# Attention outputs with the values stationary and the gate turned instead of the product

## The chip, the cores and the metric

The kernel runs on one core of a Trainium2 chip. The metric is the device time of one execution in microseconds (us). Three runs of the kernel before took 927.52, 927.58 and 927.73 us; the median is 927.58 us.

## The reference

A two-layer decoder trunk over 256 positions with a width of 2048, all f32. Each layer does the same five things; only the mixers differ.

```python
h = rmsnorm(x, norm_g)
q, k, v, ..., gate = split_cols(h @ w_in, SPLIT)
y = concatenate([mixer_1(q, k, v), mixer_2(q, k, v)])   # 16 heads of 128
x = x + (y * silu(gate)) @ w_out
```

- Layer 0: 10 heads A attend over 64 keys that a top-k search picked (one key/value head shared by all), 6 heads B over dilated windows. Both end in `softmax(logits) @ v`.
- Layer 1: 8 heads C (stick-breaking: weights `exp(log_sigmoid(z) + tail)`, not normalised) and 8 heads D (forgetting attention, a softmax).

A last RMSNorm ends the trunk. The change concerns the last steps of each head, from the weights of the keys to `y * silu(gate)`.

## The kernel before, in words

**Projections.** The 256 tokens are two blocks of 128 (`th` 0 and 1). A *job* multiplies the normed tokens by one group of columns of `w_in` or `w_out`, up to 512 wide: usually one head's q, k, v and gate, or two heads A with their gates. A job runs over 16 k-tiles of 128. To get f32 accuracy from a faster format, operands are cut into a high part (`F32R`, printed as f32 in the profile) and a low part, and each product is three matmuls: high times high, low times high, high times low (`products`, L302 to L308; 6 matmuls a k-tile). Weights come by DMA in pieces of four k-tiles; ScalarE writes their high part (`whi`, L269) and VectorE the low part (`wlo`, L270), two k-tiles (a half) at a time and three halves ahead, into four buffers.

**Order.** The schedule is written by hand: instructions reach each engine's queue in program order, and each queue runs in order. The attention of a head is a Python generator that runs beside the projection of the following job. `tick` (L293) counts projected columns. One tick is a k-tile of a 512-wide job, and two to three k-tiles of the narrow jobs K, F1 and G1 count for one or two. At each tick `advance` lets every generator whose count has run out emit its next stage; `yield n` asks for n ticks until the next one. A stage's TensorE work therefore stands between two k-tiles of the projection.

**A head.** Right after its job, ScalarE and VectorE take q, k, v and gate out of PSUM. For B (`head_b`, L484) they are rotated, and `u` is the gate times (1 + tanh). For C and D, `scaled_qk` (L649) and `vg1` (L657) scale q and k, take two exponentials, copy v, and form `u` with a reciprocal (L666) and two products (L669). C1 is the exception: its q and k come from job F1, its v and gate from job G1. Then

- q and k are turned by TensorE (`turn`, L364) and cut (`qk_turned`, L367 to L376);
- scores: one f32 matmul for the first token block, three split ones for the second (L407 to L410, L712 and L713);
- B, D and A (`softmax_head`): the masked minimum on VectorE (L414), the exponential on ScalarE (L416), three transposes of the weights (L419), a copy (L421);
- C (`stick_head`, L708): softplus, a triangular product for the running sums (L726 to L729), an exponential (L732); its weights are made turned already;
- outputs (`weigh_out`, L387): three f32 matmuls with the turned weights stationary and the values moving (L390 to L392), the product with 1/sum, norm and gate (L396), a transpose of y (L398), and the cut into `yh` and `yl` (L400, L401), from which the output projection reads.

The heads of a pair A run two ticks apart. The jobs of layer 0 are B0, K, I0, I1, B1 to B3, five pairs of A, B4 and B5, then the output projection P0 to P3. Those of layer 1 are C0, F1, G1, C2 to C7, D0 to D7, Q0 to Q3.

Of the kernel before, what the change touches and what calls it, by code (L numbers as in the profile page):

```python
# [11 lines left out]
OP = mybir.AluOpType  # L12
# [147 lines left out]
def trunk(ctx, tc, x, xT, g1, w0, wo0, w1, wo1, bf, gf, consts, rope, out):  # L160
# [216 lines left out]

    def three(o, ah, al, bh, bl):
        nc.tensor.matmul(o, ah, bh, start=True, stop=False)  # L379
        nc.tensor.matmul(o, ah, bl, start=False, stop=False)  # L380
        nc.tensor.matmul(o, al, bh, start=False, stop=True)  # L381
# [5 lines left out]
    def weigh_out(pT, vs, u, sc, kt):  # L387

        po = pa.tile([P, SEQ], F32, name="o", tag="o", bufs=1)
        nc.tensor.matmul(po[:, 0:P], pT[0], vs[0], start=True, stop=True)  # L390
        nc.tensor.matmul(po[:, P:SEQ], pT[1], vs[0], start=True, stop=False)  # L391
        nc.tensor.matmul(po[:, P:SEQ], pT[2], vs[1], start=False, stop=True)  # L392
        y = hp.tile([P, SEQ], F32, name="y", tag="y", bufs=2)
        for th in range(NT):
            t = slice(th * P, (th + 1) * P)
            nc.vector.scalar_tensor_tensor(y[:, t], po[:, t], sc[:, th:th + 1], u[:, t], op0=OP.mult, op1=OP.mult)  # L396
        yield 2 if kt == KT - 1 else 3
        pt = turn([y[:, 0:P], y[:, P:SEQ]])  # L398
        yh, yl = ys
        nc.scalar.activation(yh[:, kt, :], pt[:, 0:SEQ], AF.Copy)  # L400
        nc.vector.tensor_tensor(yl[:, kt, :], pt[:, 0:SEQ], yh[:, kt, :].bitcast(F32), op=OP.subtract)  # L401

    def softmax_head(qk, nb, vs, u, rs, kt):

        q0, k0, q1h, q1l, kh, kl = qk
        pS = pa.tile([P, 384], F32, name="s", tag="s", bufs=1)
        nc.tensor.matmul(pS[:, 0:P], q0, k0, start=True, stop=True)  # L407
        three(pS[:, P:384], q1h, q1l, kh, kl)
        sn = hp.tile([P, 384], F32, name="sn", tag="sn", bufs=2)
        nm = hp.tile([P, NT], F32, name="nm", tag="nm", bufs=2)  # L410
        pr = hp.tile([P, 384], F32, name="pr", tag="pr", bufs=2)
        l = hp.tile([P, NT], F32, name="l", tag="l", bufs=2)
        for th, s in BLK:
            nc.vector.tensor_tensor_reduce(sn[:, s], pS[:, s], nb[:, s], op0=OP.add, op1=OP.min, scale=1.0,  # L414
                                           scalar=3.0e38, accum_out=nm[:, th:th + 1])
            nc.scalar.activation(pr[:, s], sn[:, s], AF.Exp, scale=-1.0, bias=nm[:, th:th + 1],  # L416
                                 accum_out=l[:, th:th + 1])
        yield 3
        pt = turn([pr[:, 0:P], pr[:, P:SEQ], pr[:, SEQ:384]])  # L419
        pT = hp.tile([P, 384], F32, name="pT", tag="pT", bufs=2)  # L420
        nc.scalar.activation(pT, pt[:, 0:384], AF.Copy)  # L421
        sc = hp.tile([P, NT], F32, name="sc", tag="sc", bufs=2)
        nc.vector.reciprocal(sc, l)
        nc.vector.tensor_tensor(sc, sc, rs, op=OP.mult)
        yield 2
        yield from weigh_out([pT[:, i * P:(i + 1) * P] for i in range(3)], vs, u, sc, kt)
# [140 lines left out]

    def best():
# [8 lines left out]
        nc.vector.tensor_tensor(nbA, nbA, nmask, op=OP.max)  # L577

# [4 lines left out]
    def heads_a(ps, h):  # L583
# [7 lines left out]
        for th in (1, 0):  # L591
# [65 lines left out]
    def vg1(ps, o):  # L657
        v = hp.tile([P, NT, P], F32, name="v", tag="v")
        u = hp.tile([P, SEQ], F32, name="u", tag="u")
        e = hp.tile([P, SEQ], F32, name="e", tag="tg")  # L660
        for th in range(NT):
            t = slice(th * P, (th + 1) * P)
            nc.scalar.activation(e[:, t], ps[th][:, o + P:o + 256], AF.Exp, scale=nr1[:, th:th + 1])
            nc.scalar.activation(v[:, th], ps[th][:, o:o + P], AF.Copy, scale=r1[:, th:th + 1])
        nc.vector.tensor_scalar(e, e, 1.0, 3.0e38, op0=OP.add, op1=OP.min)
        nc.vector.reciprocal(e, e)  # L666
        for th in range(NT):
            t = slice(th * P, (th + 1) * P)
            nc.vector.tensor_tensor(u[:, t], ps[th][:, o + P:o + 256], e[:, t], op=OP.mult)  # L669
# [38 lines left out]
    def stick_head(qk, v, u, kt):  # L708
# [7 lines left out]
        sp = hp.tile([P, 384], F32, name="sp", tag="pr")  # L716
# [16 lines left out]
        yield 3
        yield from weigh_out([w[:, 256:384], w[:, P:256], w[:, 0:P]], [v[:, 0], v[:, 1]], u, r1, kt)

    def head_c(ps, h):
        qk = scaled_qk(ps, 0)
        v, u = vg1(ps, 256)
        yield 2
        t = qk_turned([qk[:, 384:512], qk[:, 256:384], qk[:, 0:P], qk[:, P:256]])  # L740
        yield 2
        yield from stick_head(qk_of(t), v, u, h)

    def head_cf(ps, qk):
        v, u = vg1(ps, 0)
        yield 2
        t = qk_turned([qk[:, 384:512], qk[:, 256:384], qk[:, 0:P], qk[:, P:256]])
        yield 2
        yield from stick_head(qk_of(t), v, u, 1)

    def head_d(ps, h):
# [5 lines left out]
        yield from softmax_head(qk_of(t), biases[h], [v[:, 0], v[:, 1]], u, r1, HC + h)  # L757
# [133 lines left out]
```

## Time and profile before

| | |
|---|---|
| median of the runs | 927.58 us |
| profiled execution | 927.35 us |
| its span | 925.6 us |
| TensorE busy | 916.7 us (99%) |
| VectorE busy | 591.4 us (64%) |
| ScalarE busy | 474.6 us (51%) |
| DMA | 168.77 MB, 182 GB/s over the span |

The span runs from the first to the last instruction; the profiled execution's own time contains it. "Busy" is the time in which an engine has an instruction under way. Matmuls overlap in the pipeline, so the mean of a group of matmuls (392 ns for one of 512 columns) is longer than the distance between two starts. In the timeline, starts are in us from the span's start, the second column is the duration, and x2 means two instructions merged. An f32 matmul shows as two instructions.

### The profile page before, as it was taken

Reading aid. Unit: us, or ns where it says so; the run is one execution under the profiler, and the core shown is the slowest. Engines: PE = TensorE matmul, PEld = TensorE weight load, DVE = VectorE, ACT = ScalarE, POOL = GpSimd, SP = SyncE. Lnnn points to the kernel's source line nnn. Section 1 sums busy time; section 2 is a strip of 40 time slices with the busy share of each in tenths; the row PEclk is TensorE's granted clock in tenths of the full one; section 3 lists DMA queues with packets and bytes.
Section 4 is the critical chain, followed back from the end, with each engine's and each line's share of the span. In section 5 each row is a group of like instructions: output and inputs, shape, how many; then the busy total and the mean of one; then the engine's idle time right before and its main releaser. Section 6 shows DMA issues by size and latency. Waiting matters only on the chain.

```text
span 925.6 us, 12017 instructions
## 1 busy us (share of the span) xinstructions
PE 916.7 (99%) x4541; PEld 770.8 (83%) x4541; DVE 591.4 (64%) x982; ACT 474.6 (51%) x804; POOL 48.5 (5%) x68
## 2 busy tenths in 40 slices
PE   9999999999999999999999999999999999999996
PEld 6988888888888888888898888888888888888886
DVE  7667888656666555555477666666766666665563
ACT  7645554554454455444465555555555444554450
POOL 0021100000000000000000000000000000001110
PEclk9999999999999999999999999999999999999999
DMA  9954454545444554555356454444655555455542
GB/s 359 366 189 156 164 182 166 182 154 182 141 163 153 182 181 169 187 187 186 94 204 217 183 175 156 160 158 173 236 182 188 182 167 174 176 182 182 182 182 91
DMA packets 27322, 168.77 MB, mean 182 GB/s; under 512 B 3168, under 2 KB 3712, under 8 KB 9344
## 3 DMA queue, kind: packets, MB, share of 16 engines
q1 hardware_dynamic: 25920, 164.70, 49.8%
q0 software_dynamic: 768, 2.12, 0.8%
q10 hardware_dynamic: 576, 1.19, 0.3%
q8 instruction: 35, 0.57, 0.3%
q14 instruction: 23, 0.19, 0.1%
HBM read 165.89 MB, written 2.11 MB: 182 GB/s over the span
## 4 chain that ended last, share of the span: by engine, by line
PE 97%; issue 1%; DMA 0%; DVE 0%; ACT 0%; POOL 0%; POOLq 0%; DVEq 0%; ACTq 0%
PE pj L305 30%; PE pj L306 29%; PE pj L308 29%; PE tp L364 3%; PE o L392 1%; PE o L390 1%; PE o L391 1%; PE s L407 1%; PE s L380 1%; PE s L379 1%; PE s L381 1%; DMA w0yh<-in_w_in_dram 0%; PE tp L635 0%; PE s L556 0%; PE s L557 0%
## 5 line engine op out<-in xcount | busy, mean ns | idle before, releaser
L270 DVE TENSOR_TENSOR wlo<-raw,whi 128x1024 fp32r<-128x1024 f32 (+3 forms) x300 | 356.4, 1202 | 190.7 <-ACT whi L269 189.8
L305 PE MATMUL pj<-whi,xh 128*128 128x512 f32 (+3 forms) x992 | 387.3, 392 | 0.2 <-ACT whi L269 0.2
L306 PE MATMUL pj<-whi,xl 128*128 128x512 f32 (+3 forms) x992 | 377.0, 382 | 0.0
L269 ACT ACTIVATE whi<-raw 128x1024 fp32r<-128x1024 f32 (+3 forms) x300 | 302.5, 1025 | 131.0 <-PE pj L306 125.9
L308 PE MATMUL pj<-wlo,xh 128*128 128x512 f32 (+3 forms) x992 | 297.7, 381 | 0.0
L308 PEld LDWEIGHTS pj<-wlo,xh 128*128 128x128 f32 x992 | 183.5, 188 | 36.7 <-DVE wlo L270 0.2
L305 PEld LDWEIGHTS pj<-whi,xh 128*128 128x128 f32 x992 | 186.9, 188 | 31.3 <-ACT whi L269 1.2
L306 PEld LDWEIGHTS pj<-whi,xl 128*128 128x128 f32 x992 | 187.1, 189 | 30.3
L305 PE MATMUL pj<-whi,yh 128*128 128x512 f32 (+1 forms) x248 | 96.2, 388 | 0.0
L306 PE MATMUL pj<-whi,yl 128*128 128x512 f32 (+1 forms) x248 | 94.9, 383 | 0.0
L308 PE MATMUL pj<-wlo,yh 128*128 128x512 f32 (+1 forms) x248 | 76.7, 383 | 0.0
L308 PEld LDWEIGHTS pj<-wlo,yh 128*128 128x128 f32 x248 | 46.6, 188 | 9.2
L306 PEld LDWEIGHTS pj<-whi,yl 128*128 128x128 f32 x248 | 46.7, 188 | 8.5
L305 PEld LDWEIGHTS pj<-whi,yh 128*128 128x128 f32 x248 | 46.7, 188 | 8.5
L416 ACT ACTIVATE pr<-sn,nm 128x128 f32<-128x128 f32 (+1 forms) x48 | 21.5, 449 | 47.6 <-DVE nm L414 47.6
L400 ACT ACTIVATE yh<-tp 128x256 fp32r<-128x256 f32 x32 | 12.3, 384 | 56.9 <-PE tp L364 56.7
L401 DVE TENSOR_TENSOR yl<-tp,yh 128x256 fp32r<-128x256 f32 x32 | 13.6, 424 | 26.1 <-ACT yh L400 25.3
L430 ACT ACTIVATE sq<-xs 128x512 f32<-128x512 f32 x23 | 14.3, 623 | 29.1 <-DVE xs L618 26.9
L359 POOL TENSOR_TENSOR qk<-rot,rot 128x256 f32<-128x256 f32 x22 | 15.9, 742 | 239.3 <-DVE rot L358 239.3
L666 DVE RECIPROCAL e<-e 128x256 f32<-128x256 f32 x16 | 28.0, 1753 | 0.5
L421 ACT ACTIVATE pT<-tp 128x384 f32<-128x384 f32 x24 | 11.7, 486 | 23.0 <-PE tp L364 23.0
L652 ACT ACTIVATE qk<-pj,rr 128x128 f32<-128x128 f32 x32 | 10.0, 364 | 21.3 <-PE pj L308 21.3
(207 smaller groups left out, 705.0 us busy)
## 6 DMA issues: line engine op xcount, KB each, us to landing
raw<-in_w_in_dram SPq DMA_DIRECT2D x108, 1024.0 KB, 4.8
raw<-in_w_out_dram SPq DMA_DIRECT2D x32, 1024.0 KB, 4.8
raw<-in_w_in_dram SPq DMA_DIRECT2D x4, 672.0 KB, 9.7
raw<-in_w_in_dram SPq DMA_DIRECT2D x4, 528.0 KB, 3.5
w0yl<-in_w_in_dram SPq DMA_DIRECT2D x4, 512.0 KB, 7.0
xs<-in_x_dram SPq DMA_DIRECT2D x4, 512.0 KB, 11.0
raw<-in_w_in_dram SPq DMA_DIRECT2D x4, 512.0 KB, 3.8
xst<-in_xT_dram SPq DMA_DIRECT2D x5, 256.0 KB, 6.2
```

Source lines behind the costliest of these rows:

```text
L269: nc.scalar.activation(hi, rw, AF.Copy)
L270: nc.vector.tensor_tensor(lo, rw, hi.bitcast(F32), op=OP.subtract)
L305: nc.tensor.matmul(o, a, wh, start=(kt == 0), stop=False)
L306: nc.tensor.matmul(o, b, wh, start=False, stop=False)
L308: nc.tensor.matmul(o, a, wl, start=False, stop=(kt == KT - 1))
L359: nc.gpsimd.tensor_tensor(dst, t1[:, 0:n], t2[:, 0:n], op=OP.add)
L364: nc.tensor.transpose(pt[:, i * P:(i + 1) * P], s, ident)
L400: nc.scalar.activation(yh[:, kt, :], pt[:, 0:SEQ], AF.Copy)
L401: nc.vector.tensor_tensor(yl[:, kt, :], pt[:, 0:SEQ], yh[:, kt, :].bitcast(F32), op=OP.subtract)
L416: nc.scalar.activation(pr[:, s], sn[:, s], AF.Exp, scale=-1.0, bias=nm[:, th:th + 1], accum_out=l[:, th:th + 1])
L430: nc.scalar.activation(j, xs[:, th, c * 512:(c + 1) * 512], AF.Square, accum_out=ss[:, i, th, c:c + 1])
L666: nc.vector.reciprocal(e, e)
```

## The change

- **Values stationary.** For B, C and D the output is made turned: the values of the first key block, cut into `vh` and `vl`, are stationary, and the turned weights of both token blocks, cut into `ph` and `pl`, move (three matmuls of 256 columns). The second key block matters to the second token block alone: one f32 matmul of `v1` and `p1` (128 columns).
- **Gate turned instead of y.** The output is in the layout of `yh` already, so y is no longer turned. The gate `u` is turned by TensorE and copied by ScalarE (`gate_turned`). In the softmax heads 1/sum and the norm's factor are first multiplied into `u` (`gates`); in C and D the norm's factor goes into `u` in `vg1`, in a form with two operations.
- **Places.** A softmax head now has stages at scores, +2 (gate scaled), +2 (weights and gate turned), +2 (outputs). A head C turns its gate in the stage of its q and k, 2 ticks after the head's start.
- **Pairs of A.** Both heads run in one generator and share the values (`vAs`, cut once after the search). Their weights move together: three matmuls of 512 columns and three of 256. The product and the cut cover both heads.

```diff
+    def three_of(o, ah, al, bh, bl, first, last):
+        nc.tensor.matmul(o, ah, bh, start=first, stop=False)
+        nc.tensor.matmul(o, ah, bl, start=False, stop=False)
+        nc.tensor.matmul(o, al, bh, start=False, stop=last)
...
-        nc.tensor.matmul(o, ah, bh, start=True, stop=False)
-        nc.tensor.matmul(o, ah, bl, start=False, stop=False)
-        nc.tensor.matmul(o, al, bh, start=False, stop=True)
+        three_of(o, ah, al, bh, bl, True, True)
...
-    def weigh_out(pT, vs, u, sc, kt):
+    def cut(dst, src):
+        nc.scalar.activation(dst[0], src, AF.Copy)
+        nc.vector.tensor_tensor(dst[1], src, dst[0].bitcast(F32), op=OP.subtract)
+    def values(ps, o, r, ths):
+        v = hp.tile([P, 2 * P], F32R, name="v", tag="v")
+        v1 = hp.tile([P, P], F32, name="v1", tag="v1")
+        vh, vl = v[:, 0:P], v[:, P:2 * P]
+        def upper(th):
+            nc.scalar.activation(v1 if th else vh, ps[th][:, o:o + P], AF.Copy, scale=r[:, th:th + 1])
+        def lower():
+            nc.vector.scalar_tensor_tensor(vl, ps[0][:, o:o + P], r[:, 0:1], vh.bitcast(F32),
+                                           op0=OP.mult, op1=OP.subtract)
+        for th in ths:
+            upper(th)
+        return (vh, vl, v1), upper, lower
+    def gates(u, sc):
+        for th in range(NT):
+            t = slice(th * P, (th + 1) * P)
+            nc.vector.tensor_scalar(u[:, t], u[:, t], sc[:, th:th + 1], None, op0=OP.mult)
+    def gate_turned(u, swap):
+        pt = turn([u[:, P:SEQ], u[:, 0:P]] if swap else [u[:, 0:P], u[:, P:SEQ]])
+        uT = hp.tile([P, SEQ], F32, name="uT", tag="uT")
+        nc.scalar.activation(uT, pt[:, 0:SEQ], AF.Copy)
+        return uT
+    def weigh_out(ph, pl, p1, v, uT, kt, swap):
+        vh, vl, v1 = v
...
-        nc.tensor.matmul(po[:, 0:P], pT[0], vs[0], start=True, stop=True)
-        nc.tensor.matmul(po[:, P:SEQ], pT[1], vs[0], start=True, stop=False)
-        nc.tensor.matmul(po[:, P:SEQ], pT[2], vs[1], start=False, stop=True)
-        y = hp.tile([P, SEQ], F32, name="y", tag="y", bufs=2)
-        for th in range(NT):
-            t = slice(th * P, (th + 1) * P)
-            nc.vector.scalar_tensor_tensor(y[:, t], po[:, t], sc[:, th:th + 1], u[:, t], op0=OP.mult, op1=OP.mult)
-        yield 2 if kt == KT - 1 else 3
-        pt = turn([y[:, 0:P], y[:, P:SEQ]])
+        three_of(po, vh, vl, ph, pl, True, False)
+        nc.tensor.matmul(po[:, 0:P] if swap else po[:, P:SEQ], v1, p1, start=False, stop=True)
+        y = hp.tile([P, SEQ], F32, name="y", tag="y", bufs=1)
...
-        nc.scalar.activation(yh[:, kt, :], pt[:, 0:SEQ], AF.Copy)
-        nc.vector.tensor_tensor(yl[:, kt, :], pt[:, 0:SEQ], yh[:, kt, :].bitcast(F32), op=OP.subtract)
-    def softmax_head(qk, nb, vs, u, rs, kt):
+        if swap:
+            for a, b in ((0, P), (P, 0)):
+                nc.vector.tensor_tensor(y[:, a:a + P], po[:, b:b + P], uT[:, b:b + P], op=OP.mult)
+        else:
+            nc.vector.tensor_tensor(y, po, uT, op=OP.mult)
+        cut((yh[:, kt, :], yl[:, kt, :]), y)
+    def soft(qk, nb):
...
-        pr = hp.tile([P, 384], F32, name="pr", tag="pr", bufs=2)
...
-            nc.scalar.activation(pr[:, s], sn[:, s], AF.Exp, scale=-1.0, bias=nm[:, th:th + 1],
+            nc.scalar.activation(sn[:, s], sn[:, s], AF.Exp, scale=-1.0, bias=nm[:, th:th + 1],
...
-        yield 3
-        pt = turn([pr[:, 0:P], pr[:, P:SEQ], pr[:, SEQ:384]])
-        pT = hp.tile([P, 384], F32, name="pT", tag="pT", bufs=2)
-        nc.scalar.activation(pT, pt[:, 0:384], AF.Copy)
+        return sn, l
+    def factor(l, rs):
...
-        nc.vector.tensor_tensor(sc, sc, rs, op=OP.mult)
-        yield 2
-        yield from weigh_out([pT[:, i * P:(i + 1) * P] for i in range(3)], vs, u, sc, kt)
+        if rs is not None:
+            nc.vector.tensor_tensor(sc, sc, rs, op=OP.mult)
+        return sc
+    def softmax_head(qk, nb, v, u, rs, kt):
+        pr, l = soft(qk, nb)
+        yield 2
+        gates(u, factor(l, rs))
+        yield 2
+        pt = turn([pr[:, 0:P], pr[:, P:SEQ], pr[:, SEQ:384]])
+        ph = hp.tile([P, SEQ], F32R, name="ph", tag="ph", bufs=1)
+        pl = hp.tile([P, SEQ], F32R, name="pl", tag="pl", bufs=1)
+        p1 = hp.tile([P, P], F32, name="p1", tag="p1", bufs=1)
+        cut((ph, pl), pt[:, 0:SEQ])
+        nc.scalar.activation(p1, pt[:, SEQ:384], AF.Copy)
+        uT = gate_turned(u, False)
+        yield 2
+        weigh_out(ph, pl, p1, v, uT, kt, False)
...
     def head_b(ps, h):
...
-        v = hp.tile([P, NT, P], F32, name="v", tag="v")
+        v, upper, lower = values(ps, 256, r0, ())
...
-            nc.scalar.activation(v[:, o], ps[o][:, 256:384], AF.Copy, scale=r0[:, o:o + 1])
+            upper(o)
...
+        lower()
         yield 4
...
         yield 2
-        yield from softmax_head(qk_of(t), bmask, [v[:, 0], v[:, 1]], u, hr0, YPOS[f"B{h}"])
+        yield from softmax_head(qk_of(t), bmask, v, u, hr0, YPOS[f"B{h}"])
+    vAs = []
     def best():
...
+        for n in ("ikh", "ikl"):
+            vAs.append(hp.tile([P, NT, P], F32R, name="vA" + n[2], tag=n, bufs=1))
+        cut(vAs, vA)
...
         yield from a
...
-        hs = [softmax_head((f[:, js[j]], kA, hi[:, js[j]], lo[:, js[j]], kAh, kAl), nbA, [vA[:, 0], vA[:, 1]],
-                           u[:, j].rearrange("p a b -> p (a b)"), hr0, YPOS[f"A{h + j}"]) for j in range(2)]
-        start(delay(hs[1], 2))
-        yield from hs[0]
+        ph, pl = (hp.tile([P, 2, SEQ], F32R, name="pA" + n, tag="i" + n, bufs=1) for n in "hl")
+        p1h, p1l = (hp.tile([P, 2 * P], F32R, name="pB" + n, tag="v") for n in "hl")
+        def turned(j, pr):
+            pt = turn([pr[:, 0:P], pr[:, P:SEQ], pr[:, SEQ:384]])
+            cut((ph[:, j, :], pl[:, j, :]), pt[:, 0:SEQ])
+            cut((p1h[:, js[j]], p1l[:, js[j]]), pt[:, SEQ:384])
+        sm = []
+        for j in range(2):
+            sm.append(soft((f[:, js[j]], kA, hi[:, js[j]], lo[:, js[j]], kAh, kAl), nbA))
+            yield 2
+            gates(u[:, j].rearrange("p a b -> p (a b)"), factor(sm[j][1], hr0))
+        yield 1
+        turned(0, sm[0][0])
+        yield 2
+        turned(1, sm[1][0])
+        pt = turn([u[:, j, th] for j in range(2) for th in range(NT)])
+        uT = hp.tile([P, 512], F32, name="uTA", tag="rl")
+        nc.scalar.activation(uT, pt, AF.Copy)
+        yield 3
+        po = pa.tile([P, 512], F32, name="o", tag="o", bufs=1)
+        vh, vl = vAs
+        flat = lambda t: t.rearrange("p a b -> p (a b)")
+        three_of(po, vh[:, 0], vl[:, 0], flat(ph), flat(pl), True, False)
+        o1 = po.rearrange("p (a b c) -> p a b c", a=2, b=2)[:, :, 1, :]
+        three_of(o1, vh[:, 1], vl[:, 1], p1h, p1l, False, True)
+        y = hp.tile([P, 512], F32, name="yA", tag="rl")
+        nc.vector.tensor_tensor(y, po, uT, op=OP.mult)
+        kt = YPOS[f"A{h}"]
+        cut([flat(t[:, kt:kt + 2, :]) for t in ys], y)
...
         yield n
...
     def vg1(ps, o):
-        v = hp.tile([P, NT, P], F32, name="v", tag="v")
...
+        v, upper, lower = values(ps, o, r1, ())
...
-            nc.scalar.activation(v[:, th], ps[th][:, o:o + P], AF.Copy, scale=r1[:, th:th + 1])
+            upper(th)
...
-            nc.vector.tensor_tensor(u[:, t], ps[th][:, o + P:o + 256], e[:, t], op=OP.mult)
+            nc.vector.scalar_tensor_tensor(u[:, t], ps[th][:, o + P:o + 256], r1[:, th:th + 1], e[:, t],
+                                           op0=OP.mult, op1=OP.mult)
+        lower()
...
-    def stick_head(qk, v, u, kt):
+    def stick_head(qk, v, uT, kt):
...
         yield 5
...
-        w = hp.tile([P, 384], F32, name="wT", tag="pT")
-        nc.vector.tensor_tensor(w, pW, z, op=OP.add)
-        nc.scalar.activation(w, w, AF.Exp)
-        yield 3
-        yield from weigh_out([w[:, 256:384], w[:, P:256], w[:, 0:P]], [v[:, 0], v[:, 1]], u, r1, kt)
+        nc.vector.tensor_tensor(z, pW, z, op=OP.add)
+        nc.scalar.activation(z, z, AF.Exp)
+        ph = hp.tile([P, SEQ], F32R, name="ph", tag="ph", bufs=1)
+        pl = hp.tile([P, SEQ], F32R, name="pl", tag="pl", bufs=1)
+        nc.scalar.activation(ph, z[:, P:384], AF.Copy)
+        yield 1
+        nc.vector.tensor_tensor(pl, z[:, P:384], ph.bitcast(F32), op=OP.subtract)
+        yield 2
+        weigh_out(ph, pl, z[:, 0:P], v, uT, kt, True)
+    def stick(qk, v, u, kt):
+        yield 2
+        t = qk_turned([qk[:, 384:512], qk[:, 256:384], qk[:, 0:P], qk[:, P:256]])
+        uT = gate_turned(u, True)
+        yield 2
+        yield from stick_head(qk_of(t), v, uT, kt)
     def head_c(ps, h):
...
-        yield 2
-        t = qk_turned([qk[:, 384:512], qk[:, 256:384], qk[:, 0:P], qk[:, P:256]])
-        yield 2
-        yield from stick_head(qk_of(t), v, u, h)
+        yield from stick(qk, v, u, h)
     def head_cf(ps, qk):
...
-        yield 2
-        t = qk_turned([qk[:, 384:512], qk[:, 256:384], qk[:, 0:P], qk[:, P:256]])
-        yield 2
-        yield from stick_head(qk_of(t), v, u, 1)
+        yield from stick(qk, v, u, 1)
     def head_d(ps, h):
...
         yield 2
...
         yield 2
-        yield from softmax_head(qk_of(t), biases[h], [v[:, 0], v[:, 1]], u, r1, HC + h)
+        yield from softmax_head(qk_of(t), biases[h], v, u, None, HC + h)
```

## Rows read from the trace of the kernel before

**Rows 1.** The page's busy times, shares and instruction counts.

```profile
PE 916.7 (99%) x4541; PEld 770.8 (83%) x4541; DVE 591.4 (64%) x982; ACT 474.6 (51%) x804; POOL 48.5 (5%) x68
```

**Rows 2.** Waits of TensorE, its weight loads, ScalarE: total us, times, longest.

```profile
PE pj L305 <- ACT whi L269: 0.2, 1, 0.2
...
PEld s L380 <- DVE qkl L375: 0.2, 1, 0.2
...
ACT whi L269 <- PE pj L306: 125.9, 93, 2.4
```

**Rows 3.** TensorE's timeline in job P0: start us, duration us, instruction.

```profile
355.00 0.38 PE L407 MATMUL s<-qkf 128*128 128x128 f32 x2
...
355.81 0.39 PE L306 MATMUL pj<-whi,yl 128*128 128x512 f32 x1
...
356.95 0.39 PE L305 MATMUL pj<-whi,yh 128*128 128x512 f32 x1
...
358.31 0.39 PE L305 MATMUL pj<-whi,yh 128*128 128x512 f32 x1
...
362.77 0.39 PE L390 MATMUL o<-v,pT 128*128 128x128 f32 x2
...
363.68 0.39 PE L306 MATMUL pj<-whi,yl 128*128 128x512 f32 x1
```

**Rows 4.** TensorE's timeline at the q and k transposes, jobs F1, C2, C4.

```profile
463.48 0.60 PE L364 MATMUL tp<-cons,qk 128*128 128x128 f32 x4
...
490.49 0.60 PE L364 MATMUL tp<-cons,qk 128*128 128x128 f32 x4
...
539.34 0.60 PE L364 MATMUL tp<-cons,qk 128*128 128x128 f32 x4
...
540.01 0.40 PE L306 MATMUL pj<-whi,xl 128*128 128x512 f32 x1
```

**Rows 5.** VectorE's timeline of the same three heads, up to the gate.

```profile
465.10 0.49 DVE L669 TENSOR_TENSOR u<-pj,e 128x128 f32<-128x128 f32 x2
...
490.92 0.49 DVE L669 TENSOR_TENSOR u<-pj,e 128x128 f32<-128x128 f32 x2
...
538.59 1.75 DVE L666 RECIPROCAL e<-e 128x256 f32<-128x256 f32 x1
540.38 0.49 DVE L669 TENSOR_TENSOR u<-pj,e 128x128 f32<-128x128 f32 x2
```

**Rows 6.** Groups by line: busy us, mean ns of one; idle before.

```profile
L396 DVE SCALAR_TENSOR_TENSOR y<-o,sc,u 128x128 f32<-128x128 f32 x48 | 14.6, 346 | 2.4 <-PE o L392 0.2
L401 DVE TENSOR_TENSOR yl<-tp,yh 128x256 fp32r<-128x256 f32 x32 | 13.6, 424 | 26.1 <-ACT yh L400 25.3
...
L669 DVE TENSOR_TENSOR u<-pj,e 128x128 f32<-128x128 f32 x32 | 7.8, 286 | 0.6
...
L400 ACT ACTIVATE yh<-tp 128x256 fp32r<-128x256 f32 x32 | 12.3, 384 | 56.9 <-PE tp L364 56.7
```

**Rows 7.** The timeline around the one late qkl, job F1.

```profile
466.74 0.55 DVE L375 TENSOR_TENSOR qkl<-tp,qkh 128x384 fp32r<-128x384 f32 x1
...
467.34 0.19 PEld L380 LDWEIGHTS s<-qkl,qkh 128*128 128x128 f32 x1 [0.22 <-DVE qkl L375]
...
467.57 0.28 PE L381 MATMUL s<-qkh,qkl 128*128 128x256 f32 x1
...
467.69 0.28 PE L305 MATMUL pj<-whi,xh 128*128 128x264 f32 x1
```

**Rows 8.** The timeline before the output matmuls of C0, job G1.

```profile
478.17 0.52 ACT L732 ACTIVATE wT<-wT 128x384 f32<-128x384 f32 x1 [1.23 <-DVE wT L731]
...
479.25 1.29 DVE L270 TENSOR_TENSOR wlo<-raw,whi 128x512 fp32r<-128x512 f32 x2 [1.11 <-ACT whi L269]
...
479.83 0.38 PE L390 MATMUL o<-v,wT 128*128 128x128 f32 x2
```

**Rows 9.** Busy us by engine (instructions), TensorE's granted clock, 143 to 167 us.

```profile
143.00:167.00 24.00, 24.00 (x117) 20.00 (x116) 18.94 (x49) 11.69 (x20) 1.44 (x2) 1.00 0.51 175
```

More of the change, by code (lines that the diff above doesn't have):

```diff
@@ L385, in qk_of @@
         return f[:, 0:P], f[:, P:256], hi[:, 256:384], lo[:, 256:384], hi[:, 0:256], lo[:, 0:256]
-    def weigh_out(pT, vs, u, sc, kt):
-        po = pa.tile([P, SEQ], F32, name="o", tag="o", bufs=1)
-        nc.tensor.matmul(po[:, 0:P], pT[0], vs[0], start=True, stop=True)
-        nc.tensor.matmul(po[:, P:SEQ], pT[1], vs[0], start=True, stop=False)
-        nc.tensor.matmul(po[:, P:SEQ], pT[2], vs[1], start=False, stop=True)
-        y = hp.tile([P, SEQ], F32, name="y", tag="y", bufs=2)
+    def cut(dst, src):
+        nc.scalar.activation(dst[0], src, AF.Copy)
+        nc.vector.tensor_tensor(dst[1], src, dst[0].bitcast(F32), op=OP.subtract)
@@ new lines, in gate_turned @@
+    def gate_turned(u, swap):
[5 more added lines that the diff above has]
+        vh, vl, v1 = v
+        po = pa.tile([P, SEQ], F32, name="o", tag="o", bufs=1)
+        three_of(po, vh, vl, ph, pl, True, False)
+        nc.tensor.matmul(po[:, 0:P] if swap else po[:, P:SEQ], v1, p1, start=False, stop=True)
+        y = hp.tile([P, SEQ], F32, name="y", tag="y", bufs=1)
+        yh, yl = ys
+        if swap:
[4 more added lines that the diff above has]
+        cut((yh[:, kt, :], yl[:, kt, :]), y)
@@ L715, in stick_head @@
         nc.vector.tensor_tensor(z, pZ, smask, op=OP.add)
-        sp = hp.tile([P, 384], F32, name="sp", tag="pr")
+        sp = hp.tile([P, 384], F32, name="sp", tag="sp", bufs=1)
         nc.scalar.activation(sp, z, AF.Abs)
@@ L720, in stick_head @@
         nc.vector.scalar_tensor_tensor(sp, z, 0.0, sp, op0=OP.max, op1=OP.add)
-        hi, lo = sph[:, P:512], spl[:, P:512]
-        nc.scalar.activation(hi, sp, AF.Copy)
-        nc.vector.tensor_tensor(lo, sp, hi.bitcast(F32), op=OP.subtract)
+        cut((sph[:, P:512], spl[:, P:512]), sp)
         yield 5
         pW = pa.tile([P, 384], F32, name="s", tag="s", bufs=1)
-        nc.tensor.matmul(pW, tris[0], hi, start=True, stop=False)
-        nc.tensor.matmul(pW, tris[0], lo, start=False, stop=False)
+        nc.tensor.matmul(pW, tris[0], sph[:, P:512], start=True, stop=False)
+        nc.tensor.matmul(pW, tris[0], spl[:, P:512], start=False, stop=False)
         nc.tensor.matmul(pW[:, 0:256], tris[1], sph[:, 0:256], start=False, stop=False)
         nc.tensor.matmul(pW[:, 0:256], tris[1], spl[:, 0:256], start=False, stop=True)
-        w = hp.tile([P, 384], F32, name="wT", tag="pT")
-        nc.vector.tensor_tensor(w, pW, z, op=OP.add)
-        nc.scalar.activation(w, w, AF.Exp)
-        yield 3
-        yield from weigh_out([w[:, 256:384], w[:, P:256], w[:, 0:P]], [v[:, 0], v[:, 1]], u, r1, kt)
+        nc.vector.tensor_tensor(z, pW, z, op=OP.add)
[13 more added lines that the diff above has]
+        yield from stick_head(qk_of(t), v, uT, kt)
     def head_c(ps, h):
```

## The prediction

> **What bounds the kernel now.** I read the page's busy shares first. TensorE is busy in 99% of the span [rows 1], and ScalarE and VectorE are far from it. "Busy" is not yet "the bound", so next I asked whom TensorE waited for. The answer is almost nobody: behind the warm-up its matmuls waited 0.2 us for the first cut weights, and its weight loads met one late side operand, a qkl, for 0.2 us [rows 2]. So every instruction that goes from TensorE's queue shortens the run by its slot. Every wait put into that queue lengthens the run by its whole length, since no later idle stretch could absorb it.
>
> The slots therefore come from the distance between starts in TensorE's timeline, not from the mean durations, which overlap. A projection matmul of 512 columns takes a slot of 0.227 us: six of them, one k-tile, from 356.95 to 358.31 [rows 3]. The score group of a head is one f32 matmul of 128 columns and three split (fp32r) ones of 256. It starts at 355.00, and the second projection matmul behind it at 355.81. Less one slot of 0.227 that is 0.58 us [rows 3]. Inside it a 256-column one takes 0.12 us, as from 467.57 to 467.69 [rows 7], which leaves 0.22 us for the f32 one. The present output group (three f32 matmuls, L390 to L392) runs from 362.77 to the second projection matmul at 363.68. Less one slot that is 0.68 us [rows 3].
>
> **The change, part by part.**
>
> *Output matmuls, 22 heads of B, C and D.* Three f32 matmuls of 0.68 us go. Three fp32r of 256 columns and one f32 of 128 come. That is the instruction mix of the score group, in another order: 0.58 us. The gain is 0.10 us a head, 2.2 us together. Each head still has its qk transposes and two more blocks (gate instead of y), and a softmax head three for the probabilities. So the transposes' slots cancel.
>
> *Output matmuls, 5 pairs of A.* Two groups of 0.68 us (1.36) become three of 512 columns and three of 256 columns. That is 3 x 0.227 + 3 x 0.12 = 1.04 us. The gain is 0.32 us a pair, 1.6 us together. The Trainium skill ("TensorE: Matmul & The Clock Gate", "Back-to-back issue gap") gives 131 ns for a sustained 512-column matmul. By it a pair would gain 1.36 - 0.39 - 0.36 = 0.61 us, and the five 3 us, an estimate. The row of this kernel shows 0.227 us, and the sum goes by the row.
>
> Both together: 3.8 us less on the path. Bounds 3.4 to 4.0, since the order of f32 and fp32r matmuls changes and the pairs' outputs are strided.
>
> *Gate transposes of the eight C heads.* This is the step that decides. Before, u of a C head was first read by the y product, some 12 ticks after the head's start (a tick is one k-tile of 1.36 us). Now TensorE transposes u at tick 2, right behind the four qk transposes. u is the end of a chain that starts only when the projection of the head is done: scaled q and k, two exponentials, an addition, a reciprocal of 1.75 us and two products (L652 to L669). In the job from 536.6 us the reciprocal starts at 538.59 and the two products run from 540.38 to 540.87 [rows 5]. TensorE starts the qk transposes at 539.34; the second projection matmul behind them starts at 540.01. Less one slot, it is free for the gate at 539.78 [rows 4].
>
> Two things make u later. Its products gain a scalar operand, and the form with two operations takes 346 ns (L396) against 286 ns (L669) [rows 6]: 0.12 us for two. And the handover from VectorE to TensorE costs time. The one late operand in the trace shows it: qkl is written by 467.29 (466.74 + 0.55), and L381 starts at 467.57. With a slot of 0.12, L380 really ran from 467.45, 0.16 us after its operand [rows 7]. So the gate block can start at 540.87 + 0.12 + 0.16 = 541.15. TensorE waits 541.15 - 539.78 = 1.37 us.
>
> Behind that wait stand the projection's matmuls, whose operands are ready; in the row just used the ready L305 did not pass the late L380 either. Heads C2 to C7 repeat this pattern: 6 x 1.37 = 8.2 us. C0 runs beside the narrow job F1, where tick 2 comes after three short k-tiles. TensorE is free at 463.48 + 0.44 = 463.92 and u is ready at 465.59 + 0.28 = 465.87: 1.95 us. C1 had q and k scaled a job earlier, so its chain is shorter: 490.49 + 0.44 = 490.93 against 491.41 + 0.28 = 491.69, 0.76 us [rows 4, 5]. The eight waits come to 10.9 us. Bounds: without the handover and the longer products 8.7; with twice the handover 12.2.
>
> ScalarE's copy of the turned gate also waits and holds the next weight copies (whi) behind it. TensorE waits at the same time and needs them as much later, so I count nothing more. Without that cover the copy of 0.38 us [rows 6] would be the price, once a head.
>
> *Gates of the A, B and D heads.* There the gate is scaled two ticks after the scores and turned two ticks later still. u itself is 6 ticks old or more. VectorE needs the reciprocal and the scaling, under 1 us, in 2.7 us. It is most crowded in the jobs in which the top-k search runs: 18.9 of 24 us busy [rows 9]. I take 0, with up to 0.3 us for each of the three B heads there.
>
> *Cutting the turned probabilities.* The low part (pl) makes VectorE a second link behind ScalarE's copy. That is 0.38 + 0.42 us [rows 6] in the two ticks (2.7 us) before the output matmuls, and VectorE may be in a weight subtraction (two half-wide ones take 1.29 us [rows 8], so a full one about as long). 0.3 for the transposes + 0.38 + 1.3 + 0.42 = 2.4 us still fits. It is tight in one place, C0 in the narrow job G1. The exponential ends at 478.69, the copy at 479.07, a weight copy and its subtraction (already issued, 1.3 us) stand before pl, and pl is there at about 480.8. TensorE reaches the second output matmul at 479.83 + 0.12 = 479.95 [rows 8]. That is 0 to 0.85 us; I take 0.4, because TensorE's earlier wait in C0 gives the side engines some time.
>
> *Other work on ScalarE and VectorE* (low parts of the values, gate scaling, bigger cuts for the pairs) is about 1 to 2 us in a job of 24 us. The weights are cut ahead into four buffers, and ScalarE waits 125.9 us in all for TensorE to free one [rows 2]. That is the cover, and I count nothing; without it the 27 heads and pairs would cost up to 1 to 2 us each.
>
> *The end of each layer.* The last head (B5, D7) now has its output one tick earlier or later than before, and the output projection reads it at k-tile 15. Nothing there.
>
> **Sum.** The profiled execution took 927.35 us (925.6 span and 1.75 around it). 927.35 - 3.8 + 10.9 + 0.4 = 934.85 us. The median of the runs shown is 0.23 us above the profiled one, so the forecast is 935.1 us.
>
> **Rivals.**
>
> 1. *The gate is in time and the change gains what its matmuls save.* 927.58 - 3.8 = 923.8 us, faster. For it: TensorE hardly waited before, and the stage between the two transposes was set with ticks that hid every chain so far. Against it: u's chain was never one of those. The rows put its end 1.1 us behind TensorE even before the longer products. The mechanism would have to end u 1.4 us earlier, or TensorE arrive so much later. It decides from a mean wait of 0.43 us over the eight heads, (3.8 - 0.4)/8. At or below that the change is not slower: at 0.43 it gives 927.6. The Trainium skill ("TensorE: Matmul & The Clock Gate", "Step-by-step: what each phase is for") says that only weight loads are pulled ahead while matmuls keep program order; the late L380 agrees with it.
> 2. *More waits than counted.* If pl or the scaled gate of the 14 B and D heads came late by half a weight subtraction (0.6 us), 8.4 us would be added: 943.5 us. For it: VectorE does get a second link in each head. Against it: the qk cut is such a chain of two links with longer pieces (384 columns), two ticks before its matmuls, and it was late once, by 0.2 us, in 27 [rows 2].
> 3. *TensorE's clock falls in the waits.* In the stretch of [rows 9] it was granted at 1.00, the level of 2.4 GHz. But no wait of over a microsecond stands among projection matmuls before [rows 2], so no row shows what follows one. If the following two k-tiles (2.7 us) ran at the other level, 1.2 GHz, eight heads would add 22 us: 957 us. Nothing in the rows speaks for it.
>
> **How the numbers follow.** Forecast 0.77, rival 1 with a full gain 0.07, its in-between near no change 0.04, rival 2 0.10, rival 3 0.02. The likeliest case by itself reaches from 932.4 (waits of 8.7) to 938 (twice the handover, the full C0 term and some late gates). Its tails hold perhaps 0.05, so the range goes a little further towards both sides: 931.5 to 939.5. No change is what a measurement of this kernel can't tell apart, 0.2% or 1.9 us on either side: 925.7 to 929.4. Faster takes rival 1 and a bit of the in-between, 0.08; same 0.04; slower 0.88.
>
> **What would show it.** In the changed kernel's waits of TensorE (and of its weight loads) a line "transpose of u, waiting for VectorE's product" should stand with 8 entries and 9 to 12 us, the longest about 2 us in the first C head and the others 1.1 to 1.5. The C jobs should be some 1.3 us longer, the jobs with a pair of A 0.3 shorter, the D jobs 0.1 shorter. No wait for u at all, or C jobs no longer than before, would prove the prediction wrong. A long list of waits for ph, pl or the scaled gates would mean rival 2.

## The result and the profile after

The changed kernel takes 937.26 us (median, 936.99 to 937.29) against 927.65 us (927.52 to 927.86) for the kernel before. The ratio is 1.0103, with a 95% interval of 1.0085 to 1.012. The forecast was 935.1 us with a range of 931.5 to 939.5.

TensorE's share of the span fell from 99% [rows 1] to 98%, and VectorE took 4% of the chain that ended last (before: 0%, and TensorE 97%). The page's busy times after, and the shares of its chain:

```profile
PE 916.2 (98%) x4489; PEld 767.3 (82%) x4489; DVE 618.4 (66%) x1053; ACT 488.4 (52%) x859; POOL 48.5 (5%) x68
...
PE 92%; DVE 4%; ACT 2%; issue 2%; DMA 0%; POOL 0%; SPq 0%; POOLq 0%; DVEq 0%; ACTq 0%
```

TensorE's waits after (total us, times, longest; before, [rows 2], there was next to nothing):

```profile
PE tp L364 <- DVE u L755: 9.1, 8, 1.8
PE s L892 <- DVE mhalf L888: 1.2, 1, 1.2
PE pj L305 <- ACT whi L269: 0.6, 2, 0.5
PE o L380 <- DVE pl L822: 0.6, 1, 0.6
PE tp L364 <- DVE u L416: 0.2, 1, 0.2
```

The first line is the forecast one: eight transposes of the gate that waited for VectorE's product, one in each C head. The second is the warm-up of the start, which the prediction set aside. The view counts idle time behind the modelled ends of the matmuls before; by the starts the eight waits are longer, as one of them shows. TensorE in the job of C4, beside which the q, k and gate of C3 are turned:

```profile
542.77 0.60 PE L364 MATMUL tp<-cons,qk 128*128 128x128 f32 x4
544.50 0.44 PE L364 MATMUL tp<-cons,u 128*128 128x128 f32 x2 [1.14 <-DVE u L755]
544.70 0.48 PE L305 MATMUL pj<-whi,xh 128*128 128x512 f32 x1
545.01 0.40 PE L306 MATMUL pj<-whi,xl 128*128 128x512 f32 x1
```

VectorE in the same stretch:

```profile
542.05 1.75 DVE L752 RECIPROCAL e<-e 128x256 f32<-128x256 f32 x1
543.84 0.61 DVE L755 SCALAR_TENSOR_TENSOR u<-pj,rstd,e 128x128 f32<-128x128 f32 x2
```

The products end at 544.45, and only then do the gate's transposes go. In the slots of the prediction, the group of six transposes lasts from 542.77 to the second projection matmul at 545.01, less 0.227: 2.01 us (2.02 over C2 to C7). With its operand ready the group is 0.66 us (six of 0.11), so the wait is 1.35 us.

To see where the rest is, I measured each side group of TensorE in this way in both traces, and each job from its first projection matmul to that of the next job.

| | before | after | times | sum |
|---|---|---|---|---|
| output group of B, C, D | 0.68 | 0.58 | 22 | -2.2 |
| output groups of a pair of A | 1.36 | 1.05 | 5 | -1.55 |
| wait for the gate, C2 to C7 | 0 | 1.35 | 6 | +8.1 |
| the same, C0 and C1 | 0 | 1.97, 0.72 | 1, 1 | +2.7 |
| score group of D | 0.58 | 0.745 | 8 | +1.3 |
| second transposes of a pair | 0.78 | 0.98 | 5 | +1.0 |
| transposes of B2 | 0.56 | 0.92 | 1 | +0.4 |
| output group of C0 (late pl) | 0.67 | 1.42 (0.58 + 0.84) | 1 | +0.8 |
| score group in F1 [rows 7] | 0.87 | 0.58 | 1 | -0.3 |

The lines sum to 10.3 us. The span grew by 9.9: the stretches of projection between the groups are 0.8 us shorter over all jobs (at most 0.1 in one), and the first job, with the start before it, is 0.4 us longer. Jobs C3 to D0, beside which C2 to C7 run, went from 24.43 to 25.67 us; F1 grew by 1.92, G1 by 0.52, C2 by 0.61, D1 to Q0 by 0.02 to 0.04 each; the jobs beside pairs shrank by 0.11 to 0.20.

**The new late operand in D.** Both lines of the table for D and the pairs come from the side engines, which the prediction counted at nothing. TensorE's score group of D1, in the job of D2, after:

```profile
698.51 0.38 PE L444 MATMUL s<-qkf 128*128 128x128 f32 x2
698.64 0.36 PE L379 MATMUL s<-qkh 128*128 128x256 f32 x1
...
699.24 0.40 PE L305 MATMUL pj<-whi,xh 128*128 128x512 f32 x1
699.48 0.39 PE L306 MATMUL pj<-whi,xl 128*128 128x512 f32 x1
```

VectorE ahead of it, after:

```profile
696.38 0.61 DVE L755 SCALAR_TENSOR_TENSOR u<-pj,rstd,e 128x128 f32<-128x128 f32 x2
696.90 0.34 DVE L405 SCALAR_TENSOR_TENSOR v<-pj,rstd,v 128x128 fp32r<-128x128 f32 x1
697.16 1.22 DVE L270 TENSOR_TENSOR wlo<-raw,whi 128x1024 fp32r<-128x1024 f32 x1
698.29 0.55 DVE L375 TENSOR_TENSOR qkl<-tp,qkh 128x384 fp32r<-128x384 f32 x1
```

VectorE in the same place of the kernel before:

```profile
686.73 0.49 DVE L669 TENSOR_TENSOR u<-pj,e 128x128 f32<-128x128 f32 x2
687.14 1.22 DVE L270 TENSOR_TENSOR wlo<-raw,whi 128x1024 fp32r<-128x1024 f32 x1
688.27 0.55 DVE L375 TENSOR_TENSOR qkl<-tp,qkh 128x384 fp32r<-128x384 f32 x1
```

From the start of u to that of qkl it was 1.54 us, and is now 1.91: 0.11 from the longer products and 0.26 from the low part of the values (`lower`, L405), which stands in between. qkl ends at 698.84, and from L379 (698.64) to the projection (699.24) it is 0.60 us. In a kernel below where qkl is in time it is 0.44. Neither the waits of TensorE nor those of its weight loads name the eight late qkl, because the modelled end of L379 (699.00) covers the gap. Only the distance of the starts shows it.

**One PSUM tile, two readers.** ScalarE while the first head of a pair is cut (job A6), after:

```profile
261.10 0.39 ACT L392 ACTIVATE pAh<-tp 128x256 fp32r<-128x256 f32 x1 [0.28 <-PE tp L364]
263.42 0.28 ACT L392 ACTIVATE pBh<-tp 128x128 fp32r<-128x128 f32 x1 [1.93 <-DVE pAl L393]
```

VectorE there:

```profile
261.84 1.22 DVE L270 TENSOR_TENSOR wlo<-raw,whi 128x1024 fp32r<-128x1024 f32 x1
262.97 0.42 DVE L393 TENSOR_TENSOR pAl<-tp,pAh 128x256 fp32r<-128x256 f32 x1
263.73 0.29 DVE L393 TENSOR_TENSOR pBl<-tp,pBh 128x128 fp32r<-128x128 f32 x1 [0.34 <-ACT pBh L392]
```

The two cuts are written as high, low, high, low. ScalarE's second copy reads only `tp`, but it waits 1.93 us until VectorE has read `tp`, and VectorE had a weight subtraction ahead. There are two such tiles, and the second head's transposes take the other. The pair's gates need this one again, which is read out only at 264.02 (263.73 + 0.29); they start at 264.17.

**pl of C0.** VectorE and TensorE in G1, after:

```profile
480.67 0.69 DVE L270 TENSOR_TENSOR wlo<-raw,whi 128x512 fp32r<-128x512 f32 x1 [1.56 <-ACT whi L269]
481.28 0.42 DVE L822 TENSOR_TENSOR pl<-z,ph 128x256 fp32r<-128x256 f32 x1
```

```profile
481.75 0.38 PE L380 MATMUL o<-pl,v 128*128 128x256 f32 x1 [0.57 <-DVE pl L822]
```

VectorE was free for 1.56 us, but the weight subtraction ahead of pl in its queue waited for ScalarE's copy.

### The profile page after: what moved, and what is told of

It is laid out like the page before. It is cut to its first block, busy times and chain, and to the rows that moved or that the text cites. A ratio compares the mean times of both kernels' runs of the same rounds, so it can differ in the third digit from the quotient of the medians.

```text
span 935.5 us, 12005 instructions
## 1 busy us (share of the span) xinstructions
PE 916.2 (98%) x4489; PEld 767.3 (82%) x4489; DVE 618.4 (66%) x1053; ACT 488.4 (52%) x859; POOL 48.5 (5%) x68
## 4 chain that ended last, share of the span: by engine, by line
PE 92%; DVE 4%; ACT 2%; issue 2%; DMA 0%; POOL 0%; SPq 0%; POOLq 0%; DVEq 0%; ACTq 0%
PE pj L305 28%; PE pj L306 28%; PE pj L308 28%; PE tp L364 3%; DVE e L752 1%; DVE wlo L270 1%; PE s L380 1%; PE s L444 1%; PE o L430 1%; ACT whi L269 1%; DMA w0yh<-in_w_in_dram 0%; PE s L379 0%; PE o L380 0%; PE s L381 0%; ACT e L749 0%
## 5 line engine op out<-in xcount | busy, mean ns | idle before, releaser
L305 PE MATMUL pj<-whi,xh 128*128 128x512 f32 (+3 forms) x992 | 383.9, 389 | 0.6 <-ACT whi L269 0.6
L305 PEld LDWEIGHTS pj<-whi,xh 128*128 128x128 f32 x992 | 186.6, 188 | 32.8 <-ACT whi L269 1.8
L305 PE MATMUL pj<-whi,yh 128*128 128x512 f32 (+1 forms) x248 | 96.0, 387 | 0.0
L305 PEld LDWEIGHTS pj<-whi,yh 128*128 128x128 f32 x248 | 46.6, 188 | 8.7
L452 ACT ACTIVATE sn<-sn,nm 128x128 f32<-128x128 f32 (+1 forms) x48 | 21.5, 449 | 55.3 <-DVE nm L450 55.3
L392 ACT ACTIVATE yh<-y 128x256 fp32r<-128x256 f32 x22 | 9.2, 418 | 41.4 <-DVE y L437 24.0
L364 PE MATMUL tp<-cons,u 128*128 128x128 f32 x64 | 12.0, 282 | 9.4 <-DVE u L755 9.1
L738 DVE TENSOR_SCALAR qk<-pj,rstd 128x128 f32<-128x128 f32 x32 | 9.8, 347 | 16.4 <-ACT qk L737 16.4
```

Of the source, the lines that this page charges most:

```text
L305: nc.tensor.matmul(o, a, wh, start=(kt == 0), stop=False)
L364: nc.tensor.transpose(pt[:, i * P:(i + 1) * P], s, ident)
L452: nc.scalar.activation(sn[:, s], sn[:, s], AF.Exp, scale=-1.0, bias=nm[:, th:th + 1], accum_out=l[:, th:th + 1])
L738: nc.vector.tensor_scalar(qk[:, th * 256 + P:(th + 1) * 256], ps[th][:, P:256], r1[:, th:th + 1], None, op0=OP.mult)
```

## The experiments

The first three edits are each made to the changed kernel; the later ones build on the first, as told. The kernel before, run beside them, had a median of 927.57 us. My theory was that the whole loss is the late gate of the C heads, plus side engines that are late in D and in the pairs. The rivals were that the added work itself (gate transposes, cuts) costs the time wherever it stands, or that the clock falls in the waits.

**The gate turned later.**

```diff
     def stick(qk, v, u, kt):
...
-        uT = gate_turned(u, True)
         yield 2
...
         three(pZ[:, P:384], k0h, k0l, qh, ql)
+        uT = gate_turned(u, True)
```

> Only the place of the C heads' gate transposes differs from the changed kernel: behind the scores (tick 4) instead of behind the q and k transposes (tick 2). Theory (TensorE waits for u in eight heads, 10.8 us together in the trace of the changed kernel): the waits go, 937.3 - 10.8 = 926.5 us; up to 0.8 us of that can come back in the narrow jobs F1 and G1, where TensorE no longer loses 2 us and the side engines have less time, so 926.5 to 927.3, about the time of the kernel before. Rival (turning the gate and copying it costs that time wherever it stands, by two more transposes and a copy ahead of the weight copies): 936 to 937.3. In the trace: no wait of a transpose for u in a C head.

Measured 928.22 us (927.89 to 929.45), ratio 1.0008 [0.9999, 1.0017]. TensorE's waits in this kernel, of which none is for u in a C head:

```profile
PE s L892 <- DVE mhalf L888: 1.2, 1, 1.2
PE o L380 <- DVE pl L823: 0.6, 1, 0.6
PE s L380 <- DVE qkl L375: 0.2, 1, 0.2
PE pj L305 <- ACT whi L269: 0.2, 1, 0.2
PE tp L364 <- DVE u L416: 0.2, 1, 0.2
```

So the place of two transposes accounts for 9.0 of the 9.6 us lost. The result lies 0.9 us above the expectation: TensorE now comes to the scores 1.35 us earlier, and the late qkl of D hits the C heads too. In C2 to C7 the scores with the gate last 0.95 to 0.97 us where 0.80 (0.58 + 0.22) was due, in F1 (C0) 1.31; in C1 they are at 0.80.

**The same place, an operand that is ready.** Here the C heads turn their scaled q and k in place of u, so that they aren't multiplied by their gates.

```diff
-        uT = gate_turned(u, True)
+        uT = gate_turned(qk, True)
```

> The C heads' gate transposes stay where they are (tick 2) and keep their number, copy and readers, but they read the scaled q and k, which are ready, in place of u; so the C heads are not multiplied by their gates. Theory (the wait is for u alone): as late gate, 926.5 to 927.3 us, and the six transposes of a C head take 0.66 us instead of 2.02. Rival (the place is what costs, six transposes and a third copy at once): no change, 936 to 937.3 us.

Measured 926.92 us (926.74 to 927.45), ratio 0.9993 [0.9984, 1.0002]. The six transposes take 0.66 us, and all work is still there: each engine has as many instructions as in the changed kernel. The scores of C2 to C7 stay at 0.58 us here, since the two transposes ahead of them bring TensorE to them 0.2 us later than with the late gate (3.40 us behind the first transpose instead of 3.18 to 3.22). The added transposes cost no more than their slots: the rival of the work itself falls, and what cost time was the lateness of u.

**The gate's chain longer.** A second reciprocal of e into a tile that nobody reads, ahead of the products, in C heads.

```diff
         nc.vector.reciprocal(e, e)
+        if more:
+            x = hp.tile([P, 512], F32, name="xr", tag="rt2")
+            nc.vector.reciprocal(x[:, 0:SEQ], e)
```

> One more reciprocal of 256 columns (1.75 us, its result is not read) stands in the C heads' gate chain ahead of the two products; nothing else differs from the changed kernel. Theory (TensorE stands still for as long as u is late, with no cover left): 8 x 1.75 = 14.0 us more, 951.3 us, within 1 us; the six transposes of a C head take 3.77 us instead of 2.02. Rival (the wait is only partly u's, and the rest a copy or a PSUM buffer that comes free at its own time): clearly less than 14, under 945 us.

Measured 952.49 us (951.21 to 954.8), ratio 1.027 [1.0256, 1.0284]. From the start of the first reciprocal to the end of u it is 3.97 us instead of 2.40: 1.57 more, since the second reciprocal starts 1.79 us after the first and the products only 1.67 us after the second, and these take 0.51. VectorE ahead of the gate of C3, and TensorE's waits for u in all eight heads (9.1 us in the changed kernel):

```profile
549.25 1.75 DVE L752 RECIPROCAL e<-e 128x256 f32<-128x256 f32 x1
...
552.71 0.51 DVE L758 SCALAR_TENSOR_TENSOR u<-pj,rstd,e 128x128 f32<-128x128 f32 x2
```

```profile
PE tp L364 <- DVE u L758: 21.6, 8, 3.3
```

In C3 to C7 the six transposes went from 2.02 to 3.59 us, 1.57 more (1.50 in C1). There the wait follows VectorE's chain one to one. The result lies 1.2 us above the expected 951.3 and outside its 1 us: the added reciprocal costs 1.57 us in the chain and not 1.75, and something else came on top. Eight times 1.57 is 12.6 of the 15.2 us. Almost all of the other 2.7 came in two places, F1 (2.92 us longer than in the changed kernel) and the job C3 (2.87), where TensorE's clock fell behind the wait. The windows of this kernel around it (PE, PEld, DVE, ACT and POOL busy us; then the granted clock, DMA share, GB/s), in the job C3 and then in the job C4:

```profile
524.00:526.00 2.00, 1.27 (x4) 1.15 (x5) 2.00 (x6) 0.55 (x2) 0.00 (x0) 0.54 0.00 0
526.00:528.00 2.00, 2.00 (x7) 1.56 (x6) 1.71 (x3) 0.79 (x1) 0.00 (x0) 0.60 0.47 78
528.00:530.00 2.00, 2.00 (x13) 1.74 (x12) 0.20 (x2) 0.00 (x0) 0.00 (x0) 1.00 0.96 397
...
553.00:555.00 2.00, 1.73 (x9) 1.47 (x10) 2.00 (x4) 1.25 (x2) 0.00 (x0) 1.00 0.00 0
```

TensorE's timeline there:

```profile
524.73 0.69 PE L364 MATMUL tp<-cons,u 128*128 128x128 f32 x2 [2.71 <-DVE u L758]
...
525.64 0.63 PE L306 MATMUL pj<-whi,xl 128*128 128x512 f32 x1
526.07 0.63 PE L305 MATMUL pj<-whi,xh 128*128 128x512 f32 x1
...
527.69 0.39 PE L305 MATMUL pj<-whi,xh 128*128 128x512 f32 x1
...
553.27 0.44 PE L364 MATMUL tp<-cons,u 128*128 128x128 f32 x2 [2.71 <-DVE u L758]
```

From 525.64 on the slots are 0.43 us instead of 0.227: the level of 1.2 GHz. At 527.69 a matmul is back at its usual 0.39. That cost some 1.3 us each time (2.92 and 2.87 less 1.57). In the job C4 the engine stood idle for the same 2.71 us, and the clock stayed at 1.00; so it did in the four jobs after it, with the same idle time. Why it fell behind one of these six stretches and not behind the others stays open.

**The low part of the values later.** On top of the gate turned later, C and D form it behind the cut of their q and k.

```diff
     def vg1(ps, o):
...
-        lower()
-        return v, u
+        return v, u, lower
...
         t = qk_turned([qk[:, 384:512], qk[:, 256:384], qk[:, 0:P], qk[:, P:256]])
+        lower()
```

> As the late gate, and the low part of the values of C and D is formed on VectorE behind the cut of q and k instead of ahead of it (tick 2). Theory for the part of the loss outside the C heads: that 0.34 us product makes qkl late, and the eight D heads' score groups take 0.745 us instead of 0.58. Moved, they take 0.58: 8 x 0.165 = 1.3 us less than the late gate alone, 925.2 to 926 us. Rival (the D jobs stopped gaining because of the new output group itself): no difference to the late gate, 926.5 to 927.3 us.

Measured 925.59 us (925.27 to 925.94), ratio 0.9978 [0.9969, 0.9987], 2.6 us below the kernel without this edit. VectorE in the job of D2, in this kernel, and then TensorE:

```profile
686.32 1.22 DVE L270 TENSOR_TENSOR wlo<-raw,whi 128x1024 fp32r<-128x1024 f32 x1
687.46 0.55 DVE L375 TENSOR_TENSOR qkl<-tp,qkh 128x384 fp32r<-128x384 f32 x1
687.92 0.34 DVE L405 SCALAR_TENSOR_TENSOR v<-pj,rstd,v 128x128 fp32r<-128x128 f32 x1
```

```profile
688.06 0.36 PE L379 MATMUL s<-qkh 128*128 128x256 f32 x1
...
688.50 0.40 PE L305 MATMUL pj<-whi,xh 128*128 128x512 f32 x1
```

The same instruction of 0.34 us stands behind qkl and costs nothing: the score groups of D are back at 0.58, those of C2 to C7 with the gate at 0.80. By the jobs of the two traces, D's eight are 0.17 to 0.22 us shorter each (1.5 together), those beside C2 to C7 0.15 to 0.19 (1.05), F1 is 0.2 shorter and G1 0.1 longer. The forecast of 1.3 less counted D alone; it started from 926.5 to 927.3, 0.9 us or more below what the late gate took. That 925.59 lies in its range is luck: the two misses, which come largely from the same late qkl in C, cancel.

**The pairs' cuts reordered.** On top of that, ScalarE writes both high parts, then VectorE both low ones.

```diff
-            cut((ph[:, j, :], pl[:, j, :]), pt[:, 0:SEQ])
-            cut((p1h[:, js[j]], p1l[:, js[j]]), pt[:, SEQ:384])
+            nc.scalar.activation(ph[:, j, :], pt[:, 0:SEQ], AF.Copy)
+            nc.scalar.activation(p1h[:, js[j]], pt[:, SEQ:384], AF.Copy)
+            nc.vector.tensor_tensor(pl[:, j, :], pt[:, 0:SEQ], ph[:, j, :].bitcast(F32), op=OP.subtract)
+            nc.vector.tensor_tensor(p1l[:, js[j]], pt[:, SEQ:384], p1h[:, js[j]].bitcast(F32), op=OP.subtract)
```

> As the late gate and lower part together (925.6 us), and in the pairs of A ScalarE makes both high parts of the turned weights before VectorE makes the low parts; before, the copies alternated between the two engines on one PSUM tile. Theory: the second group of transposes of a pair (0.98 us instead of 0.78) waits for that PSUM tile, which alternation keeps 0.4 us and more longer, because each engine's read of the tile waits for the other's; in the new order the group takes 0.78 us, five pairs give 1.0 us: 924.6 us. Rival (the group waits for the scaled gate of the second head on VectorE): no change, 925.6 us.

Measured 924.53 us (924.45 to 924.64), ratio 0.9967 [0.9954, 0.9979]. ScalarE's copies in this kernel follow each other, without the wait of 1.93 us:

```profile
260.53 0.39 ACT L668 ACTIVATE pAh<-tp 128x256 fp32r<-128x256 f32 x1 [0.28 <-PE tp L364]
260.81 0.27 ACT L669 ACTIVATE pBh<-tp 128x128 fp32r<-128x128 f32 x1
```

The first head's tile is read out at 263.02, before the second head's transposes start (263.08). The second transposes of a pair fell from 0.98 to 0.77, and the five jobs by 1.0 us together.

**pl and B's gates.** On top of that, C heads form pl in the stage of ph, and the gate of B and D is turned one tick behind the weights.

```diff
-        yield 1
         nc.vector.tensor_tensor(pl, z[:, P:384], ph.bitcast(F32), op=OP.subtract)
-        yield 2
+        yield 3
...
+        yield 1
         uT = gate_turned(u, False)
-        yield 2
+        yield 1
```

> As the pair order, and two more edits: in C heads the low part pl is formed in the same stage as ph (before the next weight subtraction enters VectorE's queue) instead of a tick later, and in the B and D heads the gate is turned one tick after the weights instead of with them. Theory: C0's output group in G1 falls from 1.52 to 0.58 us, B2's transposes from 0.92 to 0.55 us: 1.3 us less than the pair order alone, 923.3 us. Rival (what is cleared from one wait is taken by the next, since the side engines are that full there): above 924 us.

Measured 923.7 us (923.5 to 924.12), ratio 0.9958 [0.9945, 0.9972]. C0's output group is at 0.58 and the job B3 0.33 us shorter than in the changed kernel. The result lies 0.4 above the expectation, and below the rival's 924. Against the trace of the version ahead of it G1 is 0.92 and B3 0.35 us shorter, the 1.3 forecast; but each of the eight D jobs is 0.03 longer (0.26 together), now that its gate's transposes stand apart from those of its weights, and the first job with the start before it, which the edits don't touch, is 0.27 longer.

**C0's scores a tick later**, on top of all these:

```diff
-        yield 2
+        yield 3 if kt == 0 else 2
         yield from stick_head(qk_of(t), v, u, kt)
```

> As all, and C0's scores come a tick later, for its q and k are cut late in the narrow job F1 (the group took 1.22 us instead of 0.80). Theory: that wait of 0.4 us goes, 922.9 us. Rival (C0's later stages move a tick on and meet the work of G1): no gain or a loss, 923.3 us or more.

Measured 923.35 us (923.16 to 925.29), ratio 0.9957 [0.9945, 0.997]. Scores and gate in F1 went from 1.21 to 0.80 us, all slots. By the bounds on record this is the rival's case (923.3 or more); by the traces the wait is gone, F1 is 0.43 us shorter and G1 only 0.04 longer, and the 922.9 had started from a 923.3 that the version ahead missed by 0.4. What TensorE waits for in this kernel is the whole of this list:

```profile
PE s L895 <- DVE mhalf L891: 1.2, 1, 1.2
PE pj L305 <- ACT whi L269: 0.2, 1, 0.2
```

This is the fastest version, 4.2 us under the kernel before; its difference to the version ahead of it is within their spread.

## Why the prediction was right, and where it was off

- *The step that decides* held. Eight waits for u were forecast at 1.37 (C2 to C7), 1.95 (C0) and 0.76 us (C1), 10.9 together; they were 1.35, 1.97 and 0.72, 10.8. The longer chain adds to them one to one, and with the gate later all of them are gone. The Trainium skill ("TensorE: Matmul & The Clock Gate", "Step-by-step: what each phase is for") says that matmuls keep program order; the trace agrees: the ready L305 starts at 544.70, behind the late transposes of 544.50.
- *The output matmuls* held: 0.58 and 1.05 us against 0.58 and 1.04 forecast. With the waits gone the last version came to 923.35 us, near rival 1's 923.8: the saving of 3.8 us is real (3.75 by the table), and was only outweighed.
- *"Other work on ScalarE and VectorE ... I count nothing"* failed. The cover that I named, four weight buffers, hides work from the weights' users, not from a head's own chain: the low part of the values stands ahead of qkl in VectorE's queue, and qkl had no slack in D. Eight heads by 0.165 us: 1.3 us. So the D jobs did not become 0.1 us shorter, as forecast, but 0.02 to 0.04 longer.
- *"So the transposes' slots cancel"* held for the slots. In the pairs the order of the two engines on one PSUM tile added a wait that I hadn't looked for: 5 by 0.2, 1.0 us. So the jobs beside pairs are 0.11 to 0.20 us shorter, not 0.3.
- *Gates of the B heads*: one of three was late, B2, by 0.36 us against a bound of 0.3 (search steps stand ahead of its scaling in VectorE's queue).
- *C0's pl*: 0.84 us, at the upper bound of 0.85, where I took 0.4. TensorE's earlier wait gave VectorE time, but what stood ahead of pl waited for ScalarE.
- *Rival 2* happened in another place than it named (qkl, not pl), in eight heads instead of 14, and with 0.17 us a head instead of 0.6. *Rival 3* didn't: the granted clock was 1.00 in the wait of C3 and behind it, and fell only behind two of the waits made longer. The windows of the changed kernel, columns as above:

```profile
543.00:545.00 2.00, 0.86 (x7) 0.60 (x6) 1.96 (x5) 0.79 (x3) 0.00 (x0) 1.00 0.00 0
545.00:547.00 2.00, 2.00 (x10) 1.63 (x9) 1.96 (x3) 1.31 (x2) 0.00 (x0) 1.00 0.28 33
```

The sum was 7.5 us and the profiled executions differ by 9.9. The 2.4 between them are 1.3 (D) + 1.0 (pairs) + 0.4 (B2) + 0.4 (pl) - 0.3 (F1) - 0.8 (projections) + 0.4 (start). The start is no part of the change: the first job, the same in all these kernels, ends between 27.53 and 28.06 us in the nine traces (27.59 before, 27.96 after). The lower end of the prediction's likeliest case, 932.4, comes out only without C0's 0.4, which its words (waits of 8.7) don't say; with it, it is 932.9.

## What to carry to other kernels

When an engine without slack reads an operand earlier than before, find the end of that operand's chain and put the reader's time beside it: that one comparison gave the sign here, and the size within 2.2 us. Moving two transposes by two ticks took the loss of 1% away, and five more moves made a gain of 0.43% (0.3% to 0.55%) of it, so the places belong to such a change. An instruction added to an engine with idle time isn't free by that: here it cost 0.165 us a head ahead of the operand that the busy engine needed next, and nothing behind it. So look for late operands in the distance of starts, since the waits view can hide them behind modelled ends.

## What the runs showed that I had not expected

- Idle stretches of 1.1 to 1.8 us in TensorE, and one of 2.00 us in the kernel with the longer chain, kept the granted clock at 1.00. In that kernel it fell to the lower level behind one of 3.35 us and one of 2.71 us, and behind five others of 2.71 us it didn't. The four runs with the longer chain, 951.21 to 954.8 us, had mean granted clocks of 0.997 down to 0.991, the slowest the lowest.
- Two engines that read one PSUM tile, without writing it, were kept in program order: 1.93 us of waiting in ScalarE for a read of VectorE. No run here shows what asks for that order.
